# The S5 stage of a two-block network on one core: power tables in one run, phase tables for tile pairs, gelu before the channel shuffle, the skip term in the Toeplitz block

## The chip, the core and the metric

The kernel runs on one core of a Trainium2 chip. The metric is the device time of one execution in microseconds. Of the engines, TensorE (PE, its weight load PEld) does the matmuls, VectorE (DVE) and ScalarE (ACT) the element-wise work, GpSimd (POOL) some products, and SyncE (SP) issues most DMAs; ScalarE's queue issues the weight loads.

## The reference

Everything is 512 tokens by 2048 channels in float32. A first block has an S5 layer and a forgetting-attention layer; a second block has dilated attention and an RWKV-7 mix. Each stands between RMS norms and weight matrices of 2048 rows. The part that matters here is the S5 layer:

```python
xn = rmsnorm(h, g_pre); uz = xn @ w_in; u, z = split(uz)
# 128 groups of 16 channels, 64 complex states each; abar = exp((a_re + i a_im) dt), coef = (abar - 1) / a
x_t = coef * (B u_t)          # per group
h_t = abar * h_(t-1) + x_t    # over the 512 tokens
y_t = Re(C h_t) + d_skip * u_t
y = gelu(y); y = y * sigmoid(y @ w_glu + b_glu); y = y * silu(z)
return h + rmsnorm(y @ w_out, g_post)
```

## The kernel before

All matrices are kept transposed, channels on the 128 partitions and tokens along the row, in tiles of 128 x 512. A float32 product is made from three matmuls: weights and activations are split into a high and a low part (`wh`, `wl`, `hi`, `lo`), and `gemm` (line 206) adds hi x wh, lo x wh and hi x wl over 16 blocks, 48 matmuls a tile. It does this in four chunks of weights. Each chunk begins with a tick, which runs what `later(dt, fn)` has put down for that tick, and then with `wnext` (line 181): ScalarE starts the load of a chunk and casts it to `wh`, VectorE subtracts it to `wl` (line 192); chunks are prepared three ahead of their use.

Phase 1 (line 629) computes uz: 32 tiles, 16 of u (a "u-tile" each, 8 groups) and 16 of z (a "z-tile"). `order1` mixes them by `ZF` and `UR`: the first u-tile is at place 2 and a new one follows every 1.4 places up to place 23. Each u-tile starts its S5 work by `later`, in ticks from its first chunk (four ticks are one tile). The tokens are laid out as 8 sub-steps by 64 chunks, so that the recurrence becomes: a Toeplitz product inside eight tokens, an input product into the state of a chunk, a scan over 64 chunks, and an output product. For it the kernel needs

- once, `s5_base` (line 313): abar (`A`), coef (`C`), the rotation per chunk (`E`) and its size (`rho`);
- for every 16 groups, `s5_tables` (line 391): powers of A (`PT`), of A times C (`Q`), and of the rotation in steps of one and of eight (`e1`, `e8`), by complex products `cmul` of four VectorE operations (lines 384 to 387) through the temporary `cm`, 71 instructions per call;
- per half u-tile, `s5_pool` (tick 0 and 2): `bc` is loaded by SP and POOL makes `In` and `Ox`, three operations each; `s5_mats` (tick 6 and 8): TensorE makes the Toeplitz block `kb` and transposes `In` (`tb`), ScalarE copies them out (`Kt`, `InT`), and SP writes `Kt` in eight DMAs to `toep`;
- per u-tile, `s5_u` (behind the tile): u is scaled by `rstd`, written to HBM and read back in eight DMAs (`U`), groups on the row; `s5_phase` (tick 8): the rotation tables `Ec`, `Es`, six VectorE operations; `s5_x` (tick 10): `xb` on TensorE, nine VectorE operations with the scan; `s5_y` (tick 14): `yb` on TensorE, copied, written to HBM (`yd`), read back in eight DMAs to channels on partitions (`y`), with u read again (`ur`); `s5_gelu` (tick 18): the skip term, gelu, and the store `y2d`.

Phase 2 (line 692) loads all `y2d` tiles, splits them and runs the next matrix.

The program is written as data flow. The framework's planner puts the instructions of each engine and queue into an order by their place in the program and by its own estimate of times, and sets the waits; on the chip each queue then runs strictly in that order. Buffers come from pools: a tile with the same tag waits for an older one of `bufs` to be done.

Of the kernel before, what the change touches and what calls it, by code (L numbers as in the profile page):

```python
# [141 lines left out]
class Kern:  # L142
# [246 lines left out]
    NQ = 16  # L389

    def s5_tables(self, q, e):

        nq = self.NQ
        sl = slice(q * nq, (q + 1) * nq)
        qp = self.qp
        nc = self.nc

        def mk(s):
            return qp.tile([128, 2, 4, nq], F32, tag="cm", name="cm", bufs=2)[:, :, :s[2], :]

        A, C, E = self.s5A[:, :, sl], self.s5C[:, :, sl], self.s5E[:, :, sl]
        one = lambda t: t.unsqueeze(2)
        PT = qp.tile([128, 2, 9, nq], F32, name="PT")
        Q = qp.tile([128, 2, 8, nq], F32, name="Q")
        e1 = qp.tile([128, 2, 8, nq], F32, name="e1")
        e8 = qp.tile([128, 2, 8, nq], F32, name="e8")
        e.memset(PT[:, 0, 0, :], 1.0)
        e.memset(PT[:, 1, 0, :], 0.0)
        e.tensor_copy(PT[:, :, 1, :], A)
        self.cmul(e, PT[:, :, 2:3], PT[:, :, 1:2], PT[:, :, 1:2], [1, nq], mk)  # L410
        self.cmul(e, PT[:, :, 3:5], PT[:, :, 1:3], PT[:, :, 2:3], [2, nq], mk)
        self.cmul(e, PT[:, :, 5:9], PT[:, :, 1:5], PT[:, :, 4:5], [4, nq], mk)
        e.tensor_copy(Q[:, :, 7, :], C)
        self.cmul(e, Q[:, :, 6:7], Q[:, :, 7:8], PT[:, :, 1:2], [1, nq], mk)
        self.cmul(e, Q[:, :, 4:6], Q[:, :, 6:8], PT[:, :, 2:3], [2, nq], mk)
        self.cmul(e, Q[:, :, 0:4], Q[:, :, 4:8], PT[:, :, 4:5], [4, nq], mk)
# [1 line left out]
        e.tensor_scalar(PT[:, 0], PT[:, 0], sg, None, ALU.mult)  # L418
        e.tensor_scalar(PT[:, 1], PT[:, 1], sg, None, ALU.mult)
        e.memset(e1[:, 0, 0, :], 1.0)  # L420
        e.memset(e1[:, 1, 0, :], 0.0)
        e.memset(e8[:, 0, 0, :], 1.0)
        e.memset(e8[:, 1, 0, :], 0.0)
        e.tensor_copy(e1[:, :, 1, :], E)
        s2 = qp.tile([128, 2, 3, nq], F32, name="s2")
        self.cmul(e, s2[:, :, 0:1], e1[:, :, 1:2], e1[:, :, 1:2], [1, nq], mk)
        self.cmul(e, s2[:, :, 1:2], s2[:, :, 0:1], s2[:, :, 0:1], [1, nq], mk)
        self.cmul(e, e8[:, :, 1:2], s2[:, :, 1:2], s2[:, :, 1:2], [1, nq], mk)
        self.cmul(e, e1[:, :, 2:4], e1[:, :, 0:2], s2[:, :, 0:1], [2, nq], mk)
        self.cmul(e, e1[:, :, 4:8], e1[:, :, 0:4], s2[:, :, 1:2], [4, nq], mk)  # L430
        self.cmul(e, s2[:, :, 0:1], e8[:, :, 1:2], e8[:, :, 1:2], [1, nq], mk)
        self.cmul(e, s2[:, :, 1:2], s2[:, :, 0:1], s2[:, :, 0:1], [1, nq], mk)
# [1215 lines left out]
```

## Time and profile before

| | |
|---|---|
| time, median of 3 runs | 3324.43 us (3321.52 to 3327.26) |
| profiled execution | 3324.12 us, its span 3322.3 us |
| busy, share of the span | PE 93%, PEld 76%, DVE 62%, ACT 33%, POOL 22% |
| mean granted TensorE clock | 0.957 of full speed |
| the chain that ended last | PE 68%, DVE 19%, DMA 5%, issue 4%, SPq 2% |

The span is the time from the first to the last instruction that the profiler saw. Busy shares are means over phases with different limits: the slices of the page show VectorE at 70% or more in the first eight of forty slices and mostly far less later, and TensorE the other way. A line number is one of the kernel before.

### The profile page before, as it was taken

What the parts mean: (1) busy time and instruction counts of PE and PEld (TensorE: products, weight loads), DVE (VectorE), ACT (ScalarE), POOL (GpSimd) and SP (SyncE); (2) the same over time, 40 slices, a digit from 0 to 9 for tenths busy, and PEclk for the clock granted to TensorE, in tenths of its full rate; (3) what the DMA queues carried; (4) which work ended last, traced back from release to release, by engine and by line L of the source; (5) the groups of instructions that cost most, each with busy time, mean ns of one, the idle gap of its engine ahead of it and who ended that gap; (6) DMA issues with size and microseconds to landing.
All of it is one profiled execution on the core that took longest, in us unless ns stands there. A gap on an engine that the chain in (4) does not pass through costs nothing.

```text
span 3322.3 us, 44612 instructions
## 1 busy us (share of the span) xinstructions
PE 3105.9 (93%) x15972; PEld 2537.1 (76%) x15972; DVE 2063.0 (62%) x3715; ACT 1089.2 (33%) x1982; POOL 736.7 (22%) x677
## 2 busy tenths in 40 slices
PE   8778888999997999999999997999979999999897
PEld 6667676878886998888888885777769777777686
DVE  8999999754336723365555435578679666645634
ACT  4222222243333222243333333333312344433322
POOL 2465555111002000000000002123367310022200
PEclk9798889899998999999999998999989999999898
DMA  5234334454334433333333335445743433398543
GB/s 155 84 108 113 111 112 113 143 192 144 99 96 156 120 90 96 96 121 87 86 86 91 84 95 152 140 121 161 194 131 95 118 93 92 92 235 223 161 117 112
DMA packets 353726, 408.21 MB, mean 123 GB/s; under 512 B 138160, under 2 KB 184496, under 8 KB 353504
## 3 DMA queue, kind: packets, MB, share of 16 engines
q10 hardware_dynamic: 131328, 237.43, 25.8%
q1 hardware_dynamic: 222176, 167.93, 17.0%
q8 instruction: 126, 2.06, 0.3%
q14 instruction: 96, 0.79, 0.1%
HBM read 332.32 MB, written 64.00 MB: 119 GB/s over the span
## 4 chain that ended last, share of the span: by engine, by line
PE 68%; DVE 19%; DMA 5%; issue 4%; SPq 2%; POOL 1%; ACT 1%; DVEq 0%; ACTq 0%; POOLq 0%
PE acc L219 18%; PE acc L218 18%; PE acc L220 18%; DVE wl L192 4%; PE vb L239 2%; PE vb L238 2%; PE vb L237 2%; DMA raw<-in_w 1%; DVE Yi L1091 1%; DVE cm L384 1%; PE pt L862 1%; PE ob L879 1%; DVE w L1090 1%; SPq L1066 1%; DVE cm L385 1%
## 5 line engine op out<-in xcount | busy, mean ns | idle before, releaser
L218 PE MATMUL acc<-hi,wh 128*128 128x512 f32 x3232 | 1296.6, 402 | 29.0 <-ACT hi L169 12.6
L220 PE MATMUL acc<-hi,wl 128*128 128x512 f32 x3232 | 1296.3, 401 | 12.5 <-DVE wl L192 12.2
L219 PE MATMUL acc<-lo,wh 128*128 128x512 f32 x3232 | 1294.3, 401 | 14.4 <-DVE lo L170 11.6
L192 DVE TENSOR_TENSOR wl<-raw,wh 128x512 fp32r<-128x512 f32 (+1 forms) x912 | 685.2, 754 | 838.0 <-ACT wh L191 803.3
L191 ACT ACTIVATE wh<-raw 128x512 fp32r<-128x512 f32 (+1 forms) x912 | 570.4, 627 | 1513.4 <-PE acc L219 928.2
L218 PEld LDWEIGHTS acc<-hi,wh 128*128 128x128 f32 x3232 | 621.2, 192 | 173.6 <-ACT hi L169 14.3
L219 PEld LDWEIGHTS acc<-lo,wh 128*128 128x128 f32 x3232 | 620.7, 192 | 168.7 <-DVE lo L170 17.8
L220 PEld LDWEIGHTS acc<-hi,wl 128*128 128x128 f32 x3232 | 620.5, 192 | 156.8 <-DVE wl L192 18.8
L237 PE MATMUL vb<-wh,hi 128*128 128x256 f32 (+2 forms) x768 | 219.3, 289 | 7.0 <-ACT hi L169 5.0
L239 PE MATMUL vb<-wh,lo 128*128 128x256 f32 (+2 forms) x768 | 214.3, 290 | 9.5 <-DVE lo L170 9.5
L238 PE MATMUL vb<-wl,hi 128*128 128x256 f32 (+2 forms) x768 | 220.8, 289 | 1.3 <-DVE wl L192 1.3
L824 POOL TENSOR_TENSOR bm<-bias,cmask 128x512 f32<-128x512 f32 x16 | 21.0, 1316 | 690.2 <-DMA bias<-cumd 489.9
L237 PEld LDWEIGHTS vb<-wh,hi 128*128 128x128 f32 x768 | 148.7, 194 | 8.0 <-ACT hi L169 5.3
L239 PEld LDWEIGHTS vb<-wh,lo 128*128 128x128 f32 x768 | 145.7, 194 | 11.8 <-DVE lo L170 11.5
L238 PEld LDWEIGHTS vb<-wl,hi 128*128 128x128 f32 x768 | 149.5, 195 | 2.6 <-DVE wl L192 2.0
L730 POOL TENSOR_TENSOR y<-y,rstd 128x512 f32<-128x512 f32 x26 | 43.9, 1722 | 411.4 <-ACT rstd L288 411.4
L453 POOL TENSOR_TENSOR In<-Q,bc 128x512 f32<-128x512 f32 x32 | 52.0, 1625 | 196.9 <-DMA bc<-in_s5bc 105.9
L547 PE MATMUL yb<-H,Ox 128*128 128x63 f32 x256 | 59.8, 323 | 26.0 <-DVE H L536 26.0
L453 POOL TENSOR_TENSOR Ox<-PT,bc 128x576 f32<-128x576 f32 x32 | 53.9, 1685 | 90.8 <-DVE PT L418 56.8
L547 PEld LDWEIGHTS yb<-H,Ox 128*128 128x128 f32 x256 | 48.8, 236 | 29.4 <-DVE H L536 29.1
L1090 POOL TENSOR_TENSOR wg<-Yi 128x3 f32<-128x3 f32 (+56 forms) x114 | 65.2, 572 | 25.0 <-DVE Yi L1091 14.8
L519 PE MATMUL xb<-U,InT 128*128 128x64 f32 x256 | 44.2, 329 | 27.7 <-ACT InT L478 22.1
(435 smaller groups left out, 3601.1 us busy)
## 6 DMA issues: line engine op xcount, KB each, us to landing
raw<-in_w ACTq DMA_DIRECT2D x744, 256.0 KB
raw<-in_wk ACTq DMA_DIRECT2D x64, 256.0 KB
raw<-in_wv ACTq DMA_DIRECT2D x56, 256.0 KB
ld<-hd SPq DMA_DIRECT2D x48, 256.0 KB
ld<-y2d SPq DMA_DIRECT2D x32, 256.0 KB
hd<-h SPq DMA_DIRECT2D x32, 256.0 KB
Xd<-X SPq DMA_DIRECT2D x32, 256.0 KB
raw<-in_wd ACTq DMA_DIRECT2D x24, 256.0 KB
```

The costliest lines, as they stand in the source:

```text
L191: nc.scalar.activation(wh, raw, AF.Copy)
L192: nc.vector.tensor_sub(wl, raw, wh.bitcast(F32))
L218: nc.tensor.matmul(acc, wh[:, sl], hi, start=(kk == 0), stop=False)
L219: nc.tensor.matmul(acc, wh[:, sl], lo, start=False, stop=False)
L220: nc.tensor.matmul(acc, wl[:, sl], hi, start=False, stop=(kk == KT - 1))
L237: nc.tensor.matmul(outs[t], hi[:, tk], wh[:, sl], **st)
L238: nc.tensor.matmul(outs[t], hi[:, tk], wl[:, sl], start=False, stop=False)
L239: nc.tensor.matmul(outs[t], lo[:, tk], wh[:, sl], start=False, stop=(kk == KT - 1 and (W > 256 or t % 2 == 1)))
L453: e.tensor_tensor(o, tr, X1.unsqueeze(2).broadcast_to(shp), ALU.mult)
L519: nc.tensor.matmul(xb[:, g * 64:(g + 1) * 64], self.InT[2 * j + g // 4][:, g % 4, :], U[:, g, :], start=True, stop=True)
L547: nc.tensor.matmul(yb[:, g * 64 + 1:(g + 1) * 64], self.Ox[hb][:, g % 4, 1:9, :].rearrange("p k c -> p (k c)"), H[:, g, 0:63], start=False ...
L1090: e.tensor_tensor(w, Y[:, a:a + k, t:t + 1].broadcast_to(shp), Y[:, t:t + 1, t + 1:].broadcast_to(shp), ALU.mult)
```

## The change

Five things are changed, all in phase 1.

1. `s5_tables` runs once for all 128 groups, in eight steps that are put down for ticks 1, 3, ... 15. `e1` and `e8` hold two tiles in one row of partitions: the lower 64 partitions the groups of the even tile, the upper 64 those of the odd tile, and the powers lie next to each other in memory. The pool `sp` of the S5 work opens only at the first u-tile.
2. `s5_phase` runs for a pair of tiles at tick 6 of the even one; ScalarE copies each half to both halves of `Ec` and `Es` of its tile, the sign within the copy.
3. The skip term is added to the diagonal of the Toeplitz block: a new input `s5dd` (16 x 64 per half u-tile) is loaded by SP, and VectorE adds it to the first 16 columns of each group while `Kt` is copied from PSUM.
4. gelu is computed on `ys` in `s5_y` itself, with its two constants folded, before the channels are shuffled; the shuffle is done by eight DMAs that write `y2d`. `yd`, its reads, `ur` and `s5_gelu` go.
5. `ZF, UR` become 5 and 1.35: u-tiles at places 5 to 26. Buffers: `H` takes the one buffer of `X`, `u` and `ys` come from the common pool of eight, `InT` has three buffers, `Ec` and `Es` two.

```diff
-ZF, UR = 2, 1.4
+ZF, UR = 5, 1.35
...
+    dd = np.zeros((16, G, 16), np.float32)
+    for c in range(16):
+        dd[c, :, c] = a["s5_d"][0].reshape(G, 16)[:, c]
+    o["s5dd"] = np.ascontiguousarray(dd.reshape(16, 32, 64).transpose(1, 0, 2))
...
-    def s5_tables(self, q, e):
...
+    def s5_tables(self):
+        v, bp = self.nc.vector, self.bp
...
+            return self.b0.tile([128, 2, 4, G], F32, tag="cm", name="cm", bufs=2)[:, :, :s[2], :s[3]]
+        A, C, E = self.s5A, self.s5C, self.s5E
+        PT = bp.tile([128, 2, 9, G], F32, name="PT")
+        Q = bp.tile([128, 2, 8, G], F32, name="Q")
+        n = G // 2
+        e1t = bp.tile([128, 2, n, 8], F32, name="e1")
+        e8t = bp.tile([128, 2, n, 8], F32, name="e8")
+        e1, e8 = (t.rearrange("p i n k -> p i k n") for t in (e1t, e8t))
+        s2 = self.b0.tile([128, 2, 3, n], F32, name="s2")
+        cm = lambda out, a, b, k, w: self.cmul(v, out, a, b, [k, w], mk)
...
+        def first():
+            v.memset(PT[:, 0, 0, :], 1.0)
+            v.memset(PT[:, 1, 0, :], 0.0)
+            v.tensor_copy(PT[:, :, 1, :], A)
+            v.tensor_copy(Q[:, :, 7, :], C)
+            for t in (e1, e8):
+                v.memset(t[:, 0, 0, :], 1.0)
+                v.memset(t[:, 1, 0, :], 0.0)
+            Ev = E.rearrange("p i (m o g) -> p i m o g", o=2, g=8)
+            e1v = e1[:, :, 1, :].rearrange("p i (m g) -> p i m g", g=8)
+            for o in range(2):
+                rs = slice(64 * o, 64 * o + 64)
+                v.tensor_copy(e1v[rs], Ev[rs, :, :, o, :])
...
+        def sign():
+            for i in range(2):
+                v.tensor_scalar(PT[:, i], PT[:, i], sg, None, ALU.mult)
+        def ea():
+            cm(s2[:, :, 0:1], e1[:, :, 1:2], e1[:, :, 1:2], 1, n)
+            cm(s2[:, :, 1:2], s2[:, :, 0:1], s2[:, :, 0:1], 1, n)
+            cm(e8[:, :, 1:2], s2[:, :, 1:2], s2[:, :, 1:2], 1, n)
+            cm(e1[:, :, 2:4], e1[:, :, 0:2], s2[:, :, 0:1], 2, n)
+            cm(e1[:, :, 4:8], e1[:, :, 0:4], s2[:, :, 1:2], 4, n)
...
+        self.PT, self.Q, self.e1, self.e8 = PT, Q, e1t, e8t
+        return [first, p1, q1, p2, q2, sign, ea, eb]
     def s5_pool(self, hb):
...
-        PT, Q, e1, e8 = self.tabs[hb * 4 // self.NQ]
-        go = (hb * 4) % self.NQ
+        PT, Q, go = self.PT, self.Q, hb * 4
...
+        self.dd[hb] = sp.tile([16, 64], F32, tag="dd", name="dd", bufs=4)
+        nc.sync.dma_start(self.dd[hb], self.I["s5dd"][hb])
     def s5_mats(self, hb):
...
-        nc.scalar.activation(Kt.rearrange("p g k -> p (g k)"), kb[:16], AF.Copy)
+        k3 = kb[:16].rearrange("p (g k) -> p g k", k=128)
+        nc.scalar.activation(Kt[:, :, 16:], k3[:, :, 16:], AF.Copy)
+        nc.vector.tensor_tensor(Kt[:, :, :16], k3[:, :, :16], self.dd.pop(hb).rearrange("p (g c) -> p g c", c=16), ALU.add)
...
-        InT = sp.tile([128, 4, 128], F32, tag="InT", name="InT", bufs=4)
+        InT = sp.tile([128, 4, 128], F32, tag="InT", name="InT", bufs=3)
...
     def s5_u(self, j, acc, r):
...
-        u = sp.tile([128, 512], F32, tag="u", name="u", bufs=2)
+        u = self.tmp("u")
...
+    def s5_phase(self, m):
...
+        vw = lambda t, i, d: t[:, i, m * 8:m * 8 + 8, :].unsqueeze(d).broadcast_to(shp)
+        e1, e8 = self.e1, self.e8
+        Cc = sp.tile(shp, F32, tag="Cc", name="Cc", bufs=1)
+        Ss = sp.tile(shp, F32, tag="Ss", name="Ss", bufs=1)
...
+        v.tensor_tensor(Cc, vw(e8, 0, 3), vw(e1, 0, 2), ALU.mult)
...
+        v.tensor_tensor(Cc, Cc, et, ALU.subtract)
+        v.tensor_tensor(Ss, vw(e8, 1, 3), vw(e1, 0, 2), ALU.mult)
...
+        v.tensor_tensor(Ss, Ss, et, ALU.add)
+        Cf, Sf = (t.rearrange("p g a b -> p (g a b)") for t in (Cc, Ss))
+        for o in range(2):
+            j = 2 * m + o
+            rs = slice(64 * o, 64 * o + 64)
+            Ec = sp.tile([128, 512], F32, tag="Ec", name="Ec", bufs=2)
+            Es = sp.tile([128, 512], F32, tag="Es", name="Es", bufs=2)
+            for h in range(2):
+                hs = slice(64 * h, 64 * h + 64)
+                nc.scalar.activation(Ec[hs], Cf[rs], AF.Copy)
+                nc.scalar.activation(Es[hs], Sf[rs], AF.Copy, scale=1.0 if h == o else -1.0)
+            rt = self.rt[j % len(self.rt)]
+            nc.scalar.activation(rt[:, :, 1:], self.rho[:, j * 8:j * 8 + 8].unsqueeze(2).broadcast_to([128, 8, 63]), AF.Copy)
+            self.E[j] = Ec, Es
     def s5_x(self, j):
...
-        H = sp.tile([128, 8, 64], F32, tag="H", name="H", bufs=1)
+        H = sp.tile([128, 8, 64], F32, tag="X", name="H", bufs=1)
...
-        ys = sp.tile([128, 512], F32, tag="ys", name="ys", bufs=1)
+        ys = self.tmp("ys")
...
-    def s5_gelu(self, j):
...
+        nc.scalar.activation(q, ys, AF.Square)
+        v = nc.vector
+        v.scalar_tensor_tensor(q, q, 1 / 0.044715, ys, ALU.add, ALU.mult)
+        nc.scalar.activation(q, q, AF.Tanh, scale=0.7978845608028654 * 0.044715)
+        v.scalar_tensor_tensor(q, q, 1.0, ys, ALU.add, ALU.mult)
+        dst = self.y2d[j].rearrange("(g c) (t k) -> t c g k", c=16, k=64)
+        for t in range(8):
+            nc.sync.dma_start(dst[t], q[t * 16:(t + 1) * 16].rearrange("p (g k) -> p g k", k=64))
...
-            with tc.tile_pool(name="b0", bufs=1) as self.b0:
-                self.s5_base()
-            self.qp, self.sp = P(name="qp", bufs=2), P(name="sp", bufs=2)
-            self.tabs, self.In, self.Ox, self.InT, self.U, self.E, self.H, self.yu = ({} for _ in range(8))
-            self.tabs[0] = self.s5_tables(0, nc.vector)
-            uj = zj = 0
+            b0 = tc.tile_pool(name="b0", bufs=1)
+            self.b0 = b0.__enter__()
+            self.s5_base()
+            steps = self.s5_tables()
+            for i, f in enumerate(steps):
+                self.later(1 + 2 * i, f)
+            self.In, self.Ox, self.InT, self.U, self.E, self.H, self.dd = ({} for _ in range(7))
+            self.sp = None
...
-                    for q in range(G // self.NQ):
-                        if q not in self.tabs and q * self.NQ <= (j + 2) * 8:
-                            self.tabs[q] = self.s5_tables(q, nc.vector)
+                    if self.sp is None:
+                        while self.todo:
+                            self.tick()
+                        b0.__exit__(None, None, None)
+                        self.sp = P(name="sp", bufs=2)
                     self.later(0, self.s5_pool, 2 * j)
                     self.later(2, self.s5_pool, 2 * j + 1)
                     self.later(6, self.s5_mats, 2 * j)
                     self.later(8, self.s5_mats, 2 * j + 1)
-                    self.later(8, self.s5_phase, j)
+                    if j % 2 == 0:
+                        self.later(6, self.s5_phase, j // 2)
                     self.later(10, self.s5_x, j)
                     self.later(14, self.s5_y, j)
-                    self.later(18, self.s5_gelu, j)
```

The cut parts of `s5_tables` make the same products as before with `cm`, on G = 128 groups: `p1`, `p2` fill PT and `q1`, `q2` fill Q; `eb` fills the upper powers of `e8` as `ea` does those of `e1`. `A`, `C`, `E1` and `Esq` move from the pool bp to b0. Removed lines that the listing above shows are mostly left out.

## Rows read from the trace of the kernel before

**Rows 1.** Stretches: length, busy us (instructions) of five engines, clock, DMA share, GB/s.
```profile
16.00:73.00 57.00, 57.00 (x244) 45.76 (x244) 54.99 (x170) 30.10 (x50) 12.09 (x9) 1.00 0.48 142
73.00:543.00 470.00, 388.15 (x1899) 316.70 (x1899) 449.41 (x869) 106.40 (x185) 245.74 (x156) 0.87 0.38 107
616.00:665.00 49.00, 48.66 (x228) 40.02 (x226) 31.24 (x49) 16.83 (x28) 0.00 (x0) 1.00 0.59 178
665.00:695.00 30.00, 24.52 (x97) 19.03 (x97) 19.50 (x29) 16.49 (x28) 3.89 (x3) 0.94 0.80 271
695.00:795.00 100.00, 100.00 (x436) 81.74 (x435) 41.90 (x54) 34.17 (x55) 12.18 (x9) 1.00 0.46 144
```
**Rows 2.** Timeline of TensorE: start, duration in us, instruction, count.
```profile
317.99 1.00 PE L519 MATMUL xb<-U,InT 128*128 128x64 f32 x8
318.92 1.05 PE L467 MATMUL kb<-Ox,In 128*16 128x128 f32 x8
319.89 0.66 PE L471 MATMUL tb<-ident,In 128*128 128x128 f32 x4
...
536.41 0.33 PE L547 MATMUL yb<-H,Ox 128*128 128x63 f32 x2
...
539.48 0.39 PE L547 MATMUL yb<-H,Ox 128*128 128x63 f32 x2
...
664.73 0.40 PE L220 MATMUL acc<-hi,wl 128*128 128x512 f32 x1
```
**Rows 3.** Waits from 64 to 665 us: who for whom, total us, times, longest.
```profile
POOL In L453 <- DMA bc<-in_s5bc: 105.9, 6, 32.5
...
PE yb L547 <- DVE H L536: 26.0, 9, 7.0
...
PE xb L519 <- ACT InT L478: 22.1, 8, 10.2
PE kb L467 <- POOL Ox L455: 21.1, 11, 6.8
```
**Rows 4.** Four lines of VectorE, 64 to 665 us: ns min/median/max, first and last start.
```profile
L192 DVE TENSOR_TENSOR wl<-raw,wh x111: 664/685/1914, 66.9 to 664.0; 128x512 fp32r<-128x512 f32 x111
...
L484 DVE TENSOR_TENSOR u<-acc,rstd x16: 677/683/692, 64.1 to 536.3; 128x512 f32<-128x512 f32 x16
...
L503 DVE TENSOR_TENSOR Ec<-e,e x16: 1014/1055/2127, 87.3 to 603.1; 128x512 f32<-128x512 f32 x16
...
L530 DVE TENSOR_TENSOR_SCAN Gs<-rt,X x16: 1214/1216/2314, 114.3 to 621.6; 128x512 f32<-128x512 f32 x16
```
**Rows 5.** Timeline of VectorE.
```profile
287.87 1.72 DVE L192 TENSOR_TENSOR wl<-raw,wh 128x512 fp32r<-128x512 f32 x1
...
301.53 0.42 DVE L568 TENSOR_SCALAR q<-q 128x512 f32<-128x512 f32 x1
...
341.26 0.29 DVE L384 TENSOR_TENSOR cm<-Q,PT 128x128 f32<-128x128 f32 x1
```
**Rows 6.** Timeline of POOL.
```profile
287.14 1.90 POOL L454 TENSOR_TENSOR ptmp<-PT,bc 128x576 f32<-128x576 f32 x1
```
**Rows 7.** Groups of VectorE from 53.9 to 665 us: busy us, mean ns; idle before.
```profile
L192 DVE TENSOR_TENSOR wl<-raw,wh 128x512 fp32r<-128x512 f32 x114 | 110.4, 968 | 15.3 <-ACT wh L191 13.3 <-PE acc L219 1.8
...
L565 DVE SCALAR_TENSOR_TENSOR y<-ur,cols,y 128x512 f32<-128x512 f32 x16 | 15.5, 969 | 20.5 <-DMA toep<-Kt 12.9 <-DMA ur<-ud 4.2 <-DMA zd<-z 3.3
```
**Rows 8.** One stretch, instructions that touch `cm` alone: length, VectorE busy (count), clock.
```profile
53.90:665.00 611.10, 139.93 (x480) 0.88 0.40 113
```
**Rows 9.** Groups of VectorE from 0 to 53.9 us, wide steps of `s5_base`.
```profile
L386 DVE TENSOR_TENSOR Esq<-cmt 128x128 f32<-128x128 f32 x3 | 0.8, 279 | 0.0
...
L384 DVE TENSOR_TENSOR cmt<-Esq 128x256 f32<-128x256 f32 x2 | 0.8, 412 | 0.0
```
**Rows 10.** A group of ScalarE from 64 to 665 us: 16 partitions wide.
```profile
L473 ACT ACTIVATE Kt<-kb 16x512 f32<-16x512 f32 x32 | 18.6, 582 | 52.8 <-DVE wl L192 12.2 <-PE kb L467 7.4 <-DMA y<-yd 4.9
```
**Rows 11.** Timeline of SP's queue: eight issues in a row.
```profile
143.05 3.85 SPq L557 DMA_DIRECT2D y<-yd  x8
```

More of the change, by code (lines that the diff above doesn't have):

```diff
@@ L340, in s5_base @@
         v.tensor_scalar(th, th, 3.1415925, -3.1415925, ALU.min, ALU.max)
-        E1 = bp.tile([128, 2, G], F32, name="E1")
+        b0 = self.b0
+        E1 = b0.tile([128, 2, G], F32, name="E1")
         nc.scalar.activation(E1[:, 1, :], th, AF.Sin)
@@ L345, in s5_base @@
         v.tensor_scalar(E1[:, 0, :], k, -2.0, 1.0, ALU.mult, ALU.add)
-        A = bp.tile([128, 2, G], F32, name="A")
+        A = b0.tile([128, 2, G], F32, name="A")
         v.tensor_mul(A[:, 0, :], E1[:, 0, :], mag)
@@ L361, in s5_base @@
         v.tensor_scalar(nr, A[:, 0, :], -1.0, None, ALU.add)
-        C = bp.tile([128, 2, G], F32, name="C")
+        C = b0.tile([128, 2, G], F32, name="C")
         u = mk("u")
@@ L373, in s5_base @@
         for i in range(3):
-            En = bp.tile([128, 2, G], F32, tag="Esq", name="Esq", bufs=2)
+            En = b0.tile([128, 2, G], F32, tag="Esq", name="Esq", bufs=2)
             self.cmul(v, En, E, E, [G], lambda s: self.b0.tile(s, F32, tag="cmt", name="cmt", bufs=2))
@@ L387, in cmul @@
         e.tensor_tensor(out[:, 1], t1[:, 1], t2[:, 0], ALU.add)
-    NQ = 16
-    def s5_tables(self, q, e):
[L393 to L396, printed above, removed]
-        def mk(s):
[L399 to L416, printed above, removed]
-        sg = self.col("sg", 0)
[L418 to L432, printed above, removed]
-        self.cmul(e, e8[:, :, 2:4], e8[:, :, 0:2], s2[:, :, 0:1], [2, nq], mk)
-        self.cmul(e, e8[:, :, 4:8], e8[:, :, 0:4], s2[:, :, 1:2], [4, nq], mk)
-        return PT, Q, e1, e8
@@ new lines, in s5_tables, with p1, q1, p2 @@
+    def s5_tables(self):
+        v, bp = self.nc.vector, self.bp
+        def mk(s):
+            return self.b0.tile([128, 2, 4, G], F32, tag="cm", name="cm", bufs=2)[:, :, :s[2], :s[3]]
[8 more added lines that the diff above has]
+        cm = lambda out, a, b, k, w: self.cmul(v, out, a, b, [k, w], mk)
+        sg = self.col("sg", 0)
+        def first():
[11 more added lines that the diff above has]
+                v.tensor_copy(e1v[rs], Ev[rs, :, :, o, :])
+        def p1():
+            cm(PT[:, :, 2:3], PT[:, :, 1:2], PT[:, :, 1:2], 1, G)
+            cm(PT[:, :, 3:5], PT[:, :, 1:3], PT[:, :, 2:3], 2, G)
+        def q1():
+            cm(Q[:, :, 6:7], Q[:, :, 7:8], PT[:, :, 1:2], 1, G)
+            cm(Q[:, :, 4:6], Q[:, :, 6:8], PT[:, :, 2:3], 2, G)
+        def p2():
+            cm(PT[:, :, 5:9], PT[:, :, 1:5], PT[:, :, 4:5], 4, G)
+        def q2():
+            cm(Q[:, :, 0:4], Q[:, :, 4:8], PT[:, :, 4:5], 4, G)
+        def sign():
[7 more added lines that the diff above has]
+            cm(e1[:, :, 4:8], e1[:, :, 0:4], s2[:, :, 1:2], 4, n)
+        def eb():
+            cm(s2[:, :, 0:1], e8[:, :, 1:2], e8[:, :, 1:2], 1, n)
+            cm(s2[:, :, 1:2], s2[:, :, 0:1], s2[:, :, 0:1], 1, n)
+            cm(e8[:, :, 2:4], e8[:, :, 0:2], s2[:, :, 0:1], 2, n)
+            cm(e8[:, :, 4:8], e8[:, :, 0:4], s2[:, :, 1:2], 4, n)
+        self.PT, self.Q, self.e1, self.e8 = PT, Q, e1t, e8t
+        return [first, p1, q1, p2, q2, sign, ea, eb]
@@ L509, in s5_phase @@
-        rt = self.rt[j % len(self.rt)]
-        nc.scalar.activation(rt[:, :, 1:], self.rho[:, j * 8:j * 8 + 8].unsqueeze(2).broadcast_to([128, 8, 63]), AF.Copy)
-        self.E[j] = [t.rearrange("p g a b -> p (g a b)") for t in (Ec, Es)]
+        v.tensor_tensor(Ss, Ss, et, ALU.add)
[12 more added lines that the diff above has]
+            self.E[j] = Ec, Es
@@ L1630, in phase8 @@
             nc.sync.dma_start(self.out[k * 128:(k + 1) * 128, :], hs[k])
[L1633 removed]
+INS = ["xT", "w1", "w2", "w3", "wv0", "wv", "wk", "w5", "w6", "b_f", "cmask", "w7", "wd0", "wd", "w8", "wa2", "g2", "rope", "btab", "xmask", "chmask", "blk", "gn", "sel", "selT", "cols", "ident", "s5p", "s5bc", "s5dd"]
 def kernel(**inputs):
```

31 lines of the change are left out of this document (1 added, 30 removed).

## The prediction

> **What bounds the kernel now.** First the stretches of the span [rows 1]. From 73 to 543 us, the part of phase 1 that runs the S5 work, VectorE is busy 449.4 of 470 us and TensorE 388.2, at a granted clock of 0.87. From 695 us on, in phase 2, TensorE is busy 100 of 100 us at 1.00 and issues 436 matmuls, 0.229 us each, with VectorE at 42. So phase 1 is the part in view where TensorE is not the limit. It has 32 tiles of 48 matmuls; a tile takes 48 x 0.229 = 11.0 us when nothing holds it. Its small S5 matmuls come to 0.93 us for eight `xb`, 0.97 for eight `kb`, 0.42 for four `tb` (start to next start; for `tb` the duration less 0.24 of overlap) and 3.3 us for a whole `yb` (536.41 to 539.7) [rows 2]. One u-tile has two of each of the first three and one `yb`: 4.6 + 3.3, with a little for the breaks 8.1 us. TensorE's floor for phase 1 is then 16 us (first matmul) + 32 x 11.0 + 16 x 8.1 = 498 us; it ends at 665 [rows 2]. The 167 us between are the most that the change can win there.
>
> Second, what TensorE waited for from 64 to 665 us [rows 3]: `H` from VectorE, `InT` from ScalarE, `Ox` from POOL. POOL itself stood 106 us for `bc`, a load on SP's queue.
>
> Third, why VectorE is so full. The `wl` subtraction takes 0.664 us at best, 0.685 in the median and 1.914 at worst [rows 4]. The `wl` that began at 287.87 took 1.72 us [rows 5]; a POOL multiplication had begun at 287.14 and ended at 289.04 [rows 6], and 0.6 us later the `wl` was done. The operation `u`, with an operand in PSUM, never took more than 0.692 in 16 [rows 4]. So a VectorE operation with both operands in SBUF that meets a running POOL operation stands until that one ends, about 1 us more whatever its own size. For `wl` the mean over the median is 114 x (0.968 - 0.685) = 32 us [rows 4, 7], some 30 meetings.
>
> **The change part by part.** I work per u-tile, in the dense stretch of the order. Before, tile places 2 to 23 (22 places) hold 16 u-tiles; after, places 5 to 26, again 22. So one u-tile brings 1.375 tiles: TensorE needs 1.375 x 11.0 + 8.1 = 23.2 us at full clock. Before, the u-tiles came at 31.5 us each (64.1 to 536.3 us, 15 steps) [rows 4].
>
> VectorE before, met by no POOL operation, in issue steps (0.08 us less than a duration): `wl` 5.5 x 0.605 = 3.3; z 0.45; u 0.6; phase tables 4 x 0.95 + 2 x 0.605 = 5.0; s5_x eight x 0.62 and the scan 1.13 = 6.1; gelu 3 x 0.605 + 0.34 = 2.2 [rows 4, 5]; power tables 71 instructions per two tiles in steps of 0.07 to 0.21, about 4.1. Sum 21.8. The 9.7 us up to 31.5 are meetings and waits: 0.8 us for each of the 12 POOL products of a u-tile.
>
> *Power tables.* 8 calls of 71 instructions go. Their `cm` steps alone were 480 instructions, 139.9 us [rows 8], 16 to 128 elements wide, where a meeting costs several times the work (a 128-element one takes 0.29 us alone [rows 5]). Instead 60 such steps, eight times as wide (four times for e1 and e8), run once, in ticks 1 to 15, when POOL has no product to do. From 0.41 us for 256 elements, 0.28 for 128 [rows 9] and 0.68 for 512, about 1.05 ns an element: PT 6.4, Q 6.4, e1 and e8 9.3, signs and copies 3, together 25 us. They lie beside TensorE's first tiles; VectorE is busy 55.0 of 57 us there [rows 1], so they run late, but the first matmul that needs them is at tick 26. Bounds: 0 to 15 us late; I take 4.
>
> *Phase tables.* Six operations per tile become six per pair. The four broadcast products cost 1.01 us at best [rows 4]; with the new layout between that and 0.68, the price of a plain one: 1.8 to 2.5 us per tile; I take 2.2. New on ScalarE: four copies of 64 partitions per tile. A copy of 16 partitions took 0.58 us [rows 10], so I take 0.6 whatever the partitions, 2.4 us per tile. ScalarE is busy 106 of 470 us [rows 1], 7 us per u-tile; 10 of 27 hides, and is a wait only where the ten operations of a pair stand before a `wh` copy longer than the three prepared weight chunks last (8 us).
>
> *gelu and skip.* Two VectorE operations (the first 0.969 us in the mean [rows 7], the other at least 0.42 [rows 5]) go; 1.2 us per tile is left. On SP, a store, eight loads, a reload and a store (the eight loads 3.85 us [rows 11]) become eight stores; with two `s5dd` loads an u-tile issues 37 DMAs on SP instead of 38. The addition on `Kt`, twice, reads PSUM and is 64 elements wide: 0.15 to 0.3 us, not held by POOL (as u). New is that VectorE, ScalarE and VectorE wait for each other inside s5_y, at tick 14 instead of 18, right behind `yb`; `wl` and all else of VectorE is queued behind. Bounds 0 to 5.2 us per u-tile (`yb` 3.3, three ScalarE passes 1.9); I count it in the 2 us of wait below. `H` in the buffer of `X` makes the next X wait for `yb`, which TensorE runs before the next `xb` anyway: 0 to 3.3, I take 0. `u` in the common pool, three `InT` buffers, the later opening of the pool sp: 0 to 1 us, taken 0.
>
> The store now writes rows of 256 B, where it was 2 KB. The nearest row is the loads of the same row size, 3.85 us to issue eight [rows 11]; I hold the stores to be like them, hidden.
> The Trainium skill, "DMA: Bandwidth & Descriptors", section Specifications, says that pieces under 512 B do not reach the line rate because the engine then reads, modifies and writes. No row here shows a small store to HBM; by that rule the stores would take longer than I take them for, which is rival (C).
>
> *Sum.* VectorE after: 3.3 + 0.45 + 0.6 + 2.2 + 6.1 + 1.2 + 0.4 = 14.3 us. POOL's twelve products stay; if each again costs 0.8 us, that is 9.7 more: 24.0 us against TensorE's 23.2. VectorE no longer rules alone: both are nearly full, and neither pace will be reached. TensorE's waits from 73 to 543 are 470 - 388 = 82 us, 5.4 per u-tile, an idle share of 0.17 at clock 0.87; where it does not idle the clock is 1.00 [rows 1]. Along that line the clock is 1 - 0.76 x idle share. Two queues that are both nearly full still wait for each other; I take a good third of today's wait, 2 us: idle 0.075, clock 0.94, 23.2 / 0.94 + 2 = 26.7 us per u-tile. Phase 1 then ends at 73 (nearly five tiles, as now) + 4 + 16 x 26.7 + 5 z-tiles x 11.0 = 559 us instead of 665: 106 us less. The entry into phase 2, where 97 matmuls stand in 30 us for 131 [rows 1], hangs on loads into pages that phase 1 frees, and stays. The profiled execution took 3324.12 us (span 3322.3), 0.3 from the median 3324.43: 3324 - 106 = 3218. With waits of 1 to 3 us, 25.6 to 28.6 per u-tile, it is 3200 to 3248.
>
> **Rivals.** (A) TensorE's floor: POOL's operations fall into VectorE's gaps, few meetings are left, 24.3 us per u-tile: 73 + 389 + 55 = 517, 3176. For: VectorE's own work is 14.3 us. Against: POOL's loads still come by SP's queue.
> (B) In-line gelu: VectorE stands through `yb` and the three ScalarE passes each time, 24.0 + 5.2 = 29.2: 73 + 4 + 467 + 55 = 599, 3258. For: today's gelu comes four ticks after `yb`, and that slack is taken away. Against: the planner may put other work between.
> (C) Small stores at half speed: eight take 7.7 us instead of 3.85 [rows 11]; SP has about 18 us of issues in 27, so most hides, and the last tile's store stands before phase 2: about 4 us, 3222, inside the forecast's range.
> By the skill's rule on small pieces (the page above) this is the case that comes.
> (D) Slower: a full handover. If VectorE idles through `xb` (1.9), `yb` (3.3), the three passes (1.9), the ends of the tiles that u and z read (1) and the semaphores around them (1.5) in every u-tile, 24.0 becomes 33.6, and with tables 15 us late phase 1 ends at 73 + 15 + 538 + 55 = 681: 3340. Without the late tables it decides from 33.6 us per u-tile on. For: X and `H` share one buffer, gelu is in line. Against: the three largest waits of TensorE today are 69 us in 16 u-tiles [rows 3], and such a chain would have to be longer than VectorE's whole queue.
> (E) All meetings of the tables move to the operations that stay, one for each POOL product, 12 us: 26.3, with the waits about 28.3 per u-tile, 585, 3244: inside the forecast's range.
>
> **How the numbers follow.** Forecast with (C) and (E) 0.66, A 0.14, B 0.14, D or no gain 0.06. The predicted time is 3218. The range leaves out D and the far ends of A and B: 3172 to 3280. About 0.2% (6.6 us) is what a measurement can tell from no change: slower 0.04, within 0.02, faster 0.94.
>
> **What would show it.** In the profile after: no 16-element `cm` operations behind the first 80 us; VectorE far from 96% busy in the S5 part and TensorE's clock there above 0.9; the last matmul of phase 1 near 559 us; all later stretches of unchanged length. The forecast is wrong if u-tiles come at over 29 us, if the products of the phase tables stay at 1 us and ScalarE's copies delay `wh`, if POOL waits for `bc` more than now, or if phase 2 starts later after phase 1's end than today.

## The result and the profile after

The changed kernel takes 3239.78 us, the median of 4 runs (3236.7 to 3246.52), against 3322.97 for the kernel before beside it: ratio 0.9754, 95% interval 0.973 to 0.9778, or 83 us less. I had said 3218, with 3172 to 3280 as the range. The profiled execution took 3246.52 us, the slowest of the four (span 3244.7); the clock of its span is 0.966, before it was 0.957.

Stretches of the changed kernel, with the columns of [rows 1]:
```profile
16.00:73.00 57.00, 55.41 (x237) 44.48 (x236) 55.82 (x145) 30.87 (x52) 0.00 (x0) 1.00 0.42 133
73.00:543.00 470.00, 439.79 (x2314) 364.94 (x2314) 346.80 (x422) 175.16 (x296) 280.51 (x192) 0.93 0.40 107
543.00:600.00 57.00, 44.59 (x198) 35.27 (x198) 31.93 (x48) 21.01 (x35) 3.00 (x2) 0.82 0.58 180
600.00:700.00 100.00, 100.00 (x436) 81.75 (x436) 44.45 (x57) 34.76 (x56) 13.47 (x10) 1.00 0.47 147
```
VectorE, the third column of busy times, fell from 449 to 347 us of the 470; TensorE rose from 388 to 440, the clock from 0.87 to 0.93. The last gemm matmul of phase 1 started at 569.05 us, where it was 664.73 before [rows 2]. Phase 2 runs as before.

What waited in the changed kernel from 64 to 665 us, with the columns of [rows 3]:
```profile
POOL In L476 <- DMA bc<-in_s5bc: 228.1, 16, 100.4
...
DVE q L593 <- ACT q L591: 27.1, 12, 4.4
...
PE kb L492 <- POOL Ox L478: 13.4, 8, 5.3
...
PE yb L584 <- DVE H L573: 12.1, 6, 3.1
...
PE xb L556 <- ACT InT L506: 4.8, 2, 4.1
```
The wait for `InT` has nearly gone, the one for `H` has halved, and the second half of gelu now waits in line for ScalarE (27.1 us). POOL stands for `bc` twice as long as before, which I had named as a sign against me: 100.4 us of it are the start, before its first product; of the other 127.7, what reaches TensorE directly is the 13.4 us that it waited for `Ox`.

The lines that answer to [rows 4], 64 to 665 us (ns min/median/max, first and last start):
```profile
L196 DVE TENSOR_TENSOR wl<-raw,wh x139: 665/693/1908, 69.2 to 663.0; 128x512 fp32r<-128x512 f32 x139
...
L512 DVE TENSOR_TENSOR u<-acc,rstd x16: 668/677/692, 87.9 to 514.3; 128x512 f32<-128x512 f32 x16
...
L530 DVE TENSOR_TENSOR Cc<-e,e x8: 683/762/1618, 101.7 to 442.9; 128x512 f32<-128x512 f32 x8
...
L567 DVE TENSOR_TENSOR_SCAN Gs<-rt,X x16: 1211/1225/2454, 138.7 to 557.8; 128x512 f32<-128x512 f32 x16
```
From first to last scan there are 15 steps: (557.8 - 138.7) / 15 = 27.9 us per u-tile, where it was (621.6 - 114.3) / 15 = 33.8. By the starts of `u`, which the prediction's 31.5 goes by, it is (514.3 - 87.9) / 15 = 28.4. `u`, which reads PSUM, still never took more than 692 ns; `wl` still takes up to 1.9 us.

Instructions that touch `cm` in three stretches (length, VectorE busy and count, clock), against one stretch and 480 instructions in [rows 8]:
```profile
53.90:73.00 19.10, 11.33 (x18) 1.00 0.33 109
73.00:102.00 29.00, 16.68 (x38) 1.00 0.38 125
102.00:665.00 563.00, 0.00 (x0) 0.93 0.43 119
```

### The profile page after: what moved, and what is told of

It reads as the page before. It is cut to its first block, busy times and chain, and to the rows that moved or that the text cites. A ratio compares the mean times of both kernels' runs of the same rounds, so it can differ in the third digit from the quotient of the medians.

```text
span 3244.7 us, 44115 instructions
## 1 busy us (share of the span) xinstructions
PE 3077.6 (95%) x15972; PEld 2517.8 (78%) x15972; DVE 1889.3 (58%) x3171; ACT 1131.2 (35%) x2046; POOL 717.1 (22%) x677
## 4 chain that ended last, share of the span: by engine, by line
PE 78%; DVE 9%; POOL 4%; DMA 3%; issue 3%; SPq 2%; ACT 1%; ACTq 0%; DVEq 0%; POOLq 0%
PE acc L223 20%; PE acc L222 20%; PE acc L224 20%; PE vb L243 2%; PE vb L242 2%; PE vb L241 2%; DVE wl L196 2%; PE pt L892 1%; PE ob L909 1%; DVE Yi L1121 1%; PE xb L556 1%; PE yb L584 1%; POOL ptmp L477 1%; PE xg L1077 1%; DVE w L1120 1%
## 5 line engine op out<-in xcount | busy, mean ns | idle before, releaser
L196 DVE TENSOR_TENSOR wl<-raw,wh 128x512 fp32r<-128x512 f32 (+1 forms) x912 | 695.2, 765 | 873.5 <-ACT wh L195 841.2
L854 POOL TENSOR_TENSOR bm<-bias,cmask 128x512 f32<-128x512 f32 x16 | 21.1, 1318 | 691.6 <-DMA bias<-cumd 542.4
L476 POOL TENSOR_TENSOR In<-Q,bc 128x512 f32<-128x512 f32 x32 | 44.9, 1402 | 252.7 <-DMA bc<-in_s5bc 228.1
L1121 POOL TENSOR_TENSOR Yi<-Yi,wg 128x3 f32<-128x3 f32 (+56 forms) x114 | 60.3, 529 | 8.6
L734 POOL TENSOR_TENSOR ld<-ld 128x512 f32<-128x512 f32 x16 | 21.2, 1326 | 183.8 <-DMA ld<-zd 182.5
L1121 DVE TENSOR_TENSOR Yi<-Yi,w 128x504 f32<-128x504 f32 (+29 forms) x99 | 58.2, 612 | 5.5 <-POOL Yi L1121 4.9
```

The lines of the kernel that those rows point to most:

```text
L196: nc.vector.tensor_sub(wl, raw, wh.bitcast(F32))
L476: e.tensor_tensor(o, tr, X1.unsqueeze(2).broadcast_to(shp), ALU.mult)
L1121: e.tensor_tensor(Y[:, a:a + k, t + 1:], Y[:, a:a + k, t + 1:], w, ALU.add)
```

## The experiments

Twelve kernels were run, each with the kernel before beside it. Two theories stood at the start. T1: phase 1 is bound by VectorE's queue, and the change wins by what it takes out of it. T2: it wins by the order of the u-tiles and by what it takes off SP's queue. A price below is the difference of two ratios times 3323 us, with an uncertainty of about 9 us from their intervals; "pace" is the mean step from scan to scan. A "meeting" is counted, up to 665 us, as the excess of a VectorE instruction over the shortest of the same line and shape, where it is over 0.3 us; nearly all of these lie beside a running POOL instruction (169 of 169 us in the kernel before, 94 of 96 in the changed one).

**Undoing one part at a time.**

e1, the power tables again made for one pair of u-tiles (16 groups) at a time:
```
-    steps = self.s5_tables()          # once, [128, 2, 9, G]
+    for q in range(8):                # per pair, [128, 2, 9, 16]
+        if q not in self.tabs and q * 16 <= (j + 2) * 8:
+            self.tabs[q] = self.s5_tables(q)
```


> The kernel after, with the power tables again made for 16 groups at a time, 8 calls of some 70 small VectorE operations among the u-tiles; all else as after. Theory 1 (phase 1 was bound by VectorE's queue, and the change wins by what it takes out of it): VectorE gets back 4.1 us of its own per u-tile, from 24.0 to 28.1 us with POOL's meetings, more than TensorE's 26.9 in the profile after; some 29 us per u-tile, 16 x 2.2 = 35 us slower than after: 3275 (3262 to 3300). Theory 2 (the win is from the order of the u-tiles and the DMAs that went): 3240 to 3250.

Measured 3290.47, ratio 0.9887 (0.9868 to 0.9906): 44 us dearer than the changed kernel, as T1 had it. Pace 31.5; the meetings are 152 us, for 96 in the changed kernel, and VectorE is busy 410.54 us of the dense stretch:
```profile
73.00:543.00 470.00, 407.81 (x2055) 334.85 (x2054) 410.54 (x866) 153.46 (x262) 249.84 (x173) 0.89 0.36 96
```
The edit also brings the start of the S5 work forward (first scan at 127.3 us instead of 138.7) and moves buffers, so the 44 us stand for the tables' place and form together.

e2, the phase tables for one tile at a time, in the new layout:
```
-    for o in range(2):  j = 2 * m + o     # one call for two tiles
+    m, o = j // 2, j % 2                  # a call for each tile
```


> The kernel after, with the six VectorE operations of the phase tables made once for each tile instead of once for a pair (ScalarE's copies as after). Theory 1: 2.2 us of VectorE more per u-tile, and with 26.2 it is near TensorE's pace: 0.5 to 1.5 us per u-tile, 8 to 24 us slower than after: 3256 (3246 to 3268). Theory 2: no change, 3240.

3248.79, ratio 0.9768 (0.9755 to 0.9781): 5 us, inside the uncertainty. The time lies in T1's range, the difference under T1's 8 us, so this run does not tell T1 from T2's "no change". VectorE's busy time in the dense stretch rose by 43 us, to 389.75; the end of phase 1 came 7 us later. Work on an engine that is no longer full cost little here.

e3, gelu and skip term as before, behind the shuffle (`yd` stored, loaded as `y`, `u` reloaded):
```
-    nc.scalar.activation(ys, yb, AF.Copy); ...gelu...; 8 stores to y2d
+    yd <- ys; 8 loads y <- yd; later(18, self.s5_gelu, j)
```


> The kernel after, with the skip term and gelu again behind the shuffle (yd written and read back, u read again, four VectorE operations, one store). Theory 1: 0.6 us of VectorE and 1.4 us of its waits per u-tile come back, 5 to 25 us, and behind the last u-tile, whose chain lies open at the end of phase 1 in the profile after, a trip through HBM of 5 to 10 us more: 3262 (3248 to 3280). Theory 2 (the DMAs that went are the main win): 40 us or more, 3280 and up.

3280.19, ratio 0.9865 (0.9852 to 0.9878): 37 us, at the upper end of T1's range (3280) and at the edge of T2's (40 us or more, 3280 and up), so it does not decide between them. Pace 30.6. VectorE's queue stands for the loads (its waits from 73 to 600 us):
```profile
DVE y L597 <- DMA toep<-Kt: 20.9, 6, 5.0
...
DVE y L597 <- DMA bc<-in_s5bc: 5.8, 1, 5.8
DVE y L597 <- DMA ur<-ud: 4.8, 2, 3.5
```
These 31.5 us are VectorE waiting in line at the `y` operation, with `wl` behind it. The DMAs named are of the same SP queue, which carries the `y` loads too.

e4, the old order of the tiles (`ZF, UR = 2, 1.4` for `5, 1.35`):


> The kernel after, with the old places of the u-tiles (2 to 23 instead of 5 to 26). Theory 1: the tables come late at the start (4 to 12 us lost), the last u-tile's chain no longer lies open at the end (10 us won): 3240 (3228 to 3252). Theory 2 (the order is a main part of the win): 3265 or more.

3254.4, ratio 0.9787 (0.9773 to 0.9801): 11 us, at the edge of the uncertainty and between the two theories' numbers, but in the trace phase 2's second tile ends 13 us later as well. The first scan is at 136.0 although the u-tiles come three places earlier: something else holds it. The four parts sum to 97 us where the whole is 83; with 9 us of uncertainty on each, that difference shows nothing.

**What bounds it, before and after.** e6 and e7 leave two of the three POOL operations out of each product, in the changed kernel and in the one before:
```
     e.tensor_tensor(o, tr, X1..., ALU.mult)
-    e.tensor_tensor(t, ti, X2..., ALU.mult)
-    e.tensor_tensor(o, o, t, ALU.subtract)
```


> The kernel before with one POOL instruction for each product instead of three (the same parts left out). T1 (the kernel before is bound by VectorE's queue in phase 1, of which 169 us are excess over the shortest of the same instruction while POOL runs): without two thirds of POOL's work some 110 us of that go, and phase 1 ends near the sum of VectorE's own work and its waits, or near PE's: the time is 70 to 110 us under that of the kernel before (3215 to 3255). T2 (phase 1 is paced by the order of the u-tiles and by the loads and stores on SP's queue, which this run leaves as they are): within 25 us of the kernel before (3298 to 3325).

> The changed kernel with one POOL instruction for each product In and Ox instead of three (the imaginary part and the subtraction are left out, so the output is not the reference's): POOL's 280 us between 73 and 543 us fall to a third. Theory T1 (phase 1 is now near TensorE's own work, and of the 96 us that VectorE loses beside POOL's instructions most lies beside PE's work): PE idle between 73 us and the phase's end falls from 31.7 us to 15 to 25, the time 10 to 35 us under the changed kernel's (3205 to 3230). Rival (VectorE's meetings with POOL still set the pace): their 96 us fall to 30 to 40 and the time falls by 45 to 65 us (3175 to 3195).

e7: 3221.72, ratio 0.9686 (0.9672 to 0.9701), 101.5 us under the kernel before: T1's number, and T1 holds against T2 for the kernel before, where SP's loads, stores and order stayed as they were. The meetings fell from 169 us to 54. Its dense stretch:
```profile
73.00:543.00 470.00, 443.21 (x2356) 366.31 (x2355) 412.29 (x929) 133.61 (x229) 88.83 (x60) 0.95 0.47 132
```
POOL's own products got shorter as well, which is another way to the gain: TensorE's direct wait for `Ox` fell from 21.1 [rows 3] to 8.7 us. That is 12 us of the 101.5; what else POOL's shorter way brings is not measured.

e6: 3183.74, ratio 0.9571 (0.9558 to 0.9583), 56 us under the changed kernel by the medians, 61 by the ratios. T1's numbers for it (10 to 35) fail; the rival's come (45 to 65, meetings of 30 to 40), by which VectorE's meetings with POOL still set the pace. The stretches of e6 show where it stops:
```profile
73.00:543.00 470.00, 459.40 (x2517) 379.98 (x2516) 319.92 (x470) 196.07 (x332) 93.71 (x65) 0.98 0.48 130
543.00:600.00 57.00, 57.00 (x249) 46.60 (x248) 25.77 (x33) 20.44 (x33) 7.98 (x6) 1.00 0.47 150
```
Phase 1 ends at 520.6, and TensorE idles 5.3 us from 73 us to there; in the changed kernel it idles 31.7. That is rival A's floor (517, 3176) within 8 us. The meetings fell from 96 to 40 us, and the waits of [rows 3] with them: `kb` for `Ox` 3.9 us, `yb` for `H` none in view. But POOL's own twelve products got shorter here too, and `kb` waits for them directly (13.4 us in the changed kernel). This run doesn't separate the two.

e5, the POOL step's tiles in a pool of their own that opens ahead of the tables' scratch. I ran it because POOL's first product in the changed kernel comes late (timeline of POOL):
```profile
104.15 3.42 POOL L476 TENSOR_TENSOR In<-Q,bc 128x512 f32<-128x512 f32 x1 [100.37 <-DMA bc<-in_s5bc]
```
```
+    self.spa = P(name="spa", bufs=2)     # bc, In, Ox, ptmp, dd
     b0 = tc.tile_pool(name="b0", bufs=1)
```


> Like the changed kernel, but the tiles of the POOL step (bc, In, Ox, ptmp, dd) lie in a pool of their own that is opened before the tables' scratch, so that POOL's first product needs only its bc load and the tables PT and Q, which are done at 77.8 us, and not the end of the last table step at 101.3 us. Theory L (the tail of phase 1 is one chain of 16 u-tiles at 27.9 us from the first scan, at 136.0 us, so its start sets its end): POOL's first product at 78 to 82 us instead of 104.2, the first scan 15 to 24 us earlier, phase 1's last gemm tile at 547 to 556 us instead of 569.2, the time 12 to 24 us under the changed kernel's (3216 to 3228). Rival (the steps are paced by VectorE's queue, which has the same work in all, so an earlier start only lengthens the pace): POOL starts early too, but the last gemm tile comes at 564 to 570 us and the time is within 5 us of the changed kernel's (3235 to 3242).

3253.23, ratio 0.9786 (0.9774 to 0.9799): no gain, 13 us worse by the medians and 11 by the ratios, outside both ranges. POOL did start 31 us earlier, but the first scan came at 136.2, only 2.5 us earlier (the expectation's 136.0 for the changed kernel is misread, its row has 138.7; timelines of e5's POOL and VectorE):
```profile
73.09 3.91 POOL L476 TENSOR_TENSOR Ox<-PT,bc 128x576 f32<-128x576 f32 x2 [69.39 <-DVE PT L443]
```
```profile
97.88 1.92 DVE L389 TENSOR_TENSOR cm<-e,s 128x512 f32<-128x512 f32 x1
99.73 1.98 DVE L390 TENSOR_TENSOR cm<-e,s 128x512 f32<-128x512 f32 x1
```
The table steps now met POOL: this one takes 1.92 us, in the changed kernel 1.19, and the last ended at 116.0 instead of 101.3. What POOL won, the tables lost. Theory L falls: the start is not held by the pool alone. Phase 2's second tile is read by ScalarE at 611.19, in the changed kernel at 610.42; the rest lies behind it, in phases that the edit does not touch. There the tiles of phase 2 follow each other in 11.10 us instead of 11.05: a matmul at full clock takes 231.5 ns from step to step instead of 230.3, which over some 7600 such steps is 9 us. e1 and e8 have 231.0 ns there, some 5 us, and the other kernels 230.3 to 230.4. All three put more tiles or another pool among the buffers; whether that moves the step, and why it would, no run shows. Some 5 us of the prices of e1 and e8 may then lie behind phase 1.

e8, ten more 4 KB loads per u-tile on SP's queue:
```
+    for i in range(5):
+        xt = sp.tile([16, 64], F32, tag="xt", name="xt", bufs=6)
+        nc.sync.dma_start(xt, self.I["s5dd"][(hb + i + 1) % 32])
```


> The changed kernel with ten more loads of 4 KB on SP's queue per u-tile (five behind each dd load, into tiles that nothing reads), where it has 37. By the starts of SP's issues in a row (0.45 to 0.6 us each) that is 4.5 to 6 us more per u-tile on that queue. Theory Q (SP's in-order queue is what the S5 chain waits for, as the waits of the kernel with gelu behind the shuffle suggest, and with 28 us per u-tile it has no room left): the pace of the scans grows from 27.9 to 30 to 33 us, the time by 30 to 80 us (3270 to 3320). Rival (SP has room: some 22 us of issues in 28; what cost time there was the round trip through memory, not the number of DMAs): pace 27.9 to 28.6, time up by 0 to 12 us (3240 to 3252).

3334.81, ratio 1.0034 (1.002 to 1.0048): 93 us dearer, above even theory Q's range, all of the change's gain gone. Pace 34.3, so 0.64 us for each load:
```profile
L570 DVE TENSOR_TENSOR_SCAN Gs<-rt,X x16: 1214/1224/2247, 138.5 to 653.6; 128x512 f32<-128x512 f32 x16
```
POOL stood 340.7 us for `bc`, and TensorE 32.4 us for POOL's `Ox` (228.1 and 13.4 in the changed kernel). With 47 issues on SP's queue, its loads come late enough to pace the phase.

e9 takes the 16 `toep` stores of a u-tile off SP:
```
-    nc.sync.dma_start(Tp[...], Kt[...])            # eight
+    self.later(1, self.s5_toep, Tp, Kt, 0)         # four on nc.scalar
+    self.later(2, self.s5_toep, Tp, Kt, 4)         # four on nc.scalar
```


> The changed kernel with the 16 toep stores of a u-tile issued by ScalarE instead of SP, four each one and two weight tiles after the Kt copy. In the changed kernel SP's queue stands nearly back to back (between 299.5 and 360 us its issues leave under 1.5 us free), and eight toep stores take it 5 to 8 us. Theory Q (SP's queue paces phase 1 of the changed kernel: ten loads more cost 95 us): SP loses 10 to 16 us per u-tile, the next limit is TensorE with VectorE's meetings; pace 25 to 27 us, PE idle under 20 us, the time 20 to 55 us under the changed kernel's (3185 to 3220). Rival (the small packets are what is slow, on the shared DMA engines, and SP only waits for room there; moved to ScalarE they hold up the casts wh instead): the time within 10 us of the changed kernel's or above it (3230 to 3280).

3282.05, ratio 0.9881 (0.9864 to 0.9899): 42 us dearer, the rival's case (2 us above its range). SP's rows of the timeline from 73 us to the phase's end cover 225 us instead of 396; ScalarE's queue paid (waits of e9, 64 to 600 us; in the changed kernel the two are 3.1 and 3.0 us):
```profile
ACT wh L195 <- DMA raw<-in_w: 55.7, 29, 4.4
...
ACT wh L195 <- DMA toep<-Kt: 51.0, 16, 5.0
```
ScalarE issues the stores in line with its copies, and the weights' loads stand behind them on the same queue. So e9 does not tell whether SP's queue binds the changed kernel.

e10 and e11 do the same to e3's kernel and to the kernel before:


> The kernel with gelu and skip term as before, behind the shuffle (e3), and the toep stores issued by ScalarE as in e9. Theory Q (that part's 37 us come through SP: the round trip yd to y blocks its in-order queue and all behind it): with the queue relieved the two forms lie closer, e10 at most 15 us over e9. Rival (they come through VectorE and the round trip's own delay at the tail): e10 still 25 to 45 us over e9.

> The kernel before with its toep stores issued by ScalarE as in e9. T1 (the kernel before is bound by VectorE's queue: thin POOL products alone took 101 us): within 12 us of the kernel before, 3310 to 3335. Rival Q' (SP's queue paced the kernel before as well): 25 to 80 us less, 3240 to 3300.

e10: 3309.48, ratio 0.9965 (0.9952 to 0.9978), 28 us over e9, against 37 without the move: the rival's numbers. Most of gelu's part does not come from SP's queue, as far as a kernel with a loaded ScalarE queue can tell. The `y` waits on VectorE had shrunk from 31.5 to 4.4 us, so the round trip isn't all of it either; what makes the 28 stays open. e11: 3347.91, ratio 1.0078 (1.0064 to 1.0092), 26 us dearer than the kernel before: neither number; the move itself seems to cost here too, as in e9.

e12 was to settle SP's part: seven issues less per u-tile and nothing more elsewhere. It leaves the channel shuffle out.
```
-    for t in range(8):
-        nc.sync.dma_start(dst[t], q[t * 16:(t + 1) * 16]...)
+    nc.sync.dma_start(self.y2d[j], q)
```


> The changed kernel with q stored to y2d by one DMA of 2 KB rows per u-tile instead of eight of 256 B rows (the channel shuffle is left out, so the output is not the reference's): seven issues less per u-tile on SP's queue and nothing more on any other engine. Theory Q (SP's queue paces phase 1: ten loads more made the scans' pace 34.3 us, or 0.64 us a load): seven fewer take about 4.5 us per u-tile from it, so the pace falls to 24 to 26.5 us, the stores at the end of the phase take under 1 us instead of 3.6, and the time falls by 20 to 50 us against the changed kernel's (3190 to 3220). Rival P (the pace is that of VectorE beside POOL, as the thin products suggest with their 56 us, and SP's queue only fills up when loaded more): pace 27.4 to 28, the time 0 to 10 us under the changed kernel's (3230 to 3240).

3247.88, ratio 0.9771 (0.9754 to 0.9789): no gain, and 8 us above rival P's range. The S5 chain did run faster, at a pace of 26.8 between theory Q's 26.5 and rival P's 27.4 (e12's scans and stretch; compare 138.7 to 557.8 and 439.79 above):
```profile
L567 DVE TENSOR_TENSOR_SCAN Gs<-rt,X x16: 1215/2025/2311, 139.7 to 541.5; 128x512 f32<-128x512 f32 x16
```
```profile
73.00:543.00 470.00, 433.87 (x2278) 359.50 (x2277) 360.46 (x423) 171.35 (x292) 294.62 (x192) 0.92 0.36 106
```
The last scan came 16 us earlier, and TensorE did no more work for it: it idled 36 us up to the phase's end (`yb` for `H`: 20.1) at a clock of 0.92, and VectorE's meetings rose from 96 to 110 us. Phase 2's second tile is read at 610.66, in the changed kernel at 610.42. So taking seven of the 37 issues off does not bring phase 2 forward; adding ten puts it back.

## Why the prediction was right, point by point

**The mechanism.** VectorE's queue bound the kernel before: e7 shows it against T2, with the meetings falling by 115 us and the time by 101.5; POOL's own shorter way is a part that no run separates. Taking the tables out was the largest single part, 44 us (e1), gelu and skip 37 (e3), phase tables 5, order 11. That phase 1 would then come near TensorE's work, with neither engine at its pace, is what the trace shows: VectorE 347 of 470 us, TensorE 440. The reason given for the wait, two queues that are both nearly full, did not come: VectorE is at 74%. That the wait came out near the 2 us taken for it is then partly luck.

**VectorE per u-tile.** Forecast 24.0: 14.3 of its own and 9.7 of meetings. Measured 346.8 / 470 x 27.9 = 20.6; meetings of 96 us over 16 u-tiles are 6.0, which leaves 14.6. The own work was right. I had charged 0.8 us to each POOL product; it was 0.5; with gaps in VectorE's queue fewer of them would meet anything. Rival E, all meetings moving over, is out. Those that stay weigh on the plain operations: `wl` has a mean of 1058 ns from 73 to 569 us, over 1006 in the kernel before.

**TensorE's ledger, from 73 us to the phase's end.** Work at full clock by my terms is 27 tiles x 11.0 + 16 x 8.1 = 426.6 us. Forecast: 36 of waits (16 x 2 and 4 for the tables), 23 of clock, end 559. Measured: 31.7 of idle, 496.2 - 426.6 - 31.7 = 38 of clock and all else, end 569. The wait was right within 4 us; the clock, with all else that is left, was the mis-sized term, by 15 us. My line from idle share to clock (1 - 0.76 x share) gave 0.95 for the measured 30.2 / 470, and the granted clock was 0.93; in e3 it was 0.93 at twice that share (57 us of 470), so the line is no rule. The pace I had put at 26.7 came out at 27.9 from scan to scan, and at (569 - 73 - 4 - 55) / 16 = 27.3 in the terms of my sum. My range of 25.6 to 28.6 for waits of 1 to 3 us did not follow that line: by it the pace is 24.9 to 28.2, the time 3190 to 3242.

**Entry into phase 2: "stays".** This step failed, and with it one of my signs of being wrong came true; another, the longer wait of POOL for `bc`, came too. From the end of phase 1's last tile (its 48th matmul) to the end of the next tile was 19.1 us before, and is 29.6: 10.5 us given back. The last u-tile's `yb`, gelu and stores now stand behind the last gemm tile, and phase 2's loads behind them on SP's queue (SP and TensorE, timelines):
```profile
577.18 3.65 SPq L598 DMA_DIRECT2D y2d<-q  x8
580.93 0.86 SPq L710 DMA_DIRECT2D zd<-z  x2
581.85 11.01 SPq L719 DMA_DIRECT2D ld<-y2d  x16
```
```profile
579.83 0.79 PE L222 MATMUL acc<-hi,wh 128*128 128x512 f32 x1 [7.09 <-ACT hi L170]
585.58 0.80 PE L222 MATMUL acc<-hi,wh 128*128 128x512 f32 x1 [3.80 <-ACT hi L170]
```
The matmul after each wait takes 0.79 us, twice 0.39: the clock is at the lower of its two levels there (1.2 instead of 2.4 GHz), and its mean over that stretch is 0.82. In e4, where eight z-tiles follow the last u-tile instead of five, the same step takes 18 us, no more than before, but phase 1 ends 25 us later. So -106 became -96 at the last tile and -85 at phase 2's second tile; the rest, to the 83 of the medians, is within what runs differ by.

**Late tables: 0 to 15 us, taken 4.** They ended at 101.3 us; the 56 wide `cm` steps after 53.9 us took 28 us against 25 in my sum for all. TensorE ran through until tile 8, at 108.2; tiles 9 and 10, with the first S5 matmuls and POOL at work in a row from 104 us on, then took 22.6 and 31.1 us. "Later opening of the pool: 0 to 1" was too small for POOL's start (104 us for the `bc` load it could have had earlier), and still right for the end: in e5, with POOL 31 us earlier, phase 2's second tile came no sooner.

**Phase tables.** Products 683 at best and 762 ns in the median, for the 0.68 to 1.01 I had bounded; ScalarE's copies of 64 partitions 0.63 for my 0.6. e2 shows that it hardly mattered.

**gelu.** Bounds 0 to 5.2 us per u-tile, within the wait: VectorE stood 27.1 us in all for ScalarE's pass, 1.7 per u-tile. Rival B (29.2 us per u-tile) is out by the pace, though less clearly than I thought. The 37 us that the part is worth were not in my sum, which counted VectorE's operations alone. VectorE standing in line for `y` (31.5 us in e3) is one thing it left out, but with 4.4 us of it in e10 28 us remained, so what the part is worth is not explained.

**Rival C, small stores.** The last eight were issued in 3.65 us, as I held them to be. In the dense stretch eight span 3.7 to 7.6 us from the first issue to the end of the last, as the loads that they replace did (3.7 to 9.9 in the kernel before); the issues themselves come to 3.7 us in the median, for the loads 3.4. My 18 us of issues per u-tile on SP's queue were too few: its rows cover 396 us from 73 us to the phase's end, 25 per u-tile. One large store in place of the eight (e12) gained nothing. The Trainium skill, "DMA: Bandwidth & Descriptors", Specifications, has a rule on pieces under 512 B, by which the small stores would take longer. No run here shows it: the rows give the time to issue a store, not to land it.

**Rival D**, the handover that makes it slower, is out: 27.9 us per u-tile, not 33.6; e8 shows that a slower case was near all the same, by SP's queue: ten more issues per u-tile, and the gain is gone.

**Still open.** Of e6's 56 us, how much is fewer meetings and how much POOL's shorter way to `Ox`. Why gelu's part keeps 28 us with SP relieved (e10). What moves the matmul step of later phases in e1, e5 and e8. No kernel that computes all of the reference came out under the changed one.

## What to carry to other kernels

When an engine is full, split its busy time into work and excess over the shortest of the same instruction, and test the cause by thinning the other engine: here two thirds of POOL's operations were worth 101 us, 12 us of it seen as TensorE's direct wait for POOL. Such a test shortens the thinned engine's own chain too, so look at who waits for it. Once the bound moves to an in-order engine that is 94% busy, a faster chain beside it (e12) changed nothing at the end, but one queue with little room left (SP, e8) still took the whole gain back. Count the end of a stage as its own step: what is moved later in the order stands alone there.
